# Row standard deviation of an 8192 x 8192 matrix: bn_stats on VectorE for part of each row, and last rows in falling pieces

## Chip, cores, metric

The kernel runs on one core of one Trainium2 chip. The metric is the time of the device in microseconds, of one execution. The profile is of one execution; its span is 1.7 to 2.2 us shorter than the measured time, and all times inside a run are counted from the start of that span.

## The reference

```python
x = np.random.randn(8192, 8192).astype(np.float32)
np.std(x, axis=1)          # 8192 results
```

268 MB must be read, and 32 KB are written.

## The kernel before

Row `p*64 + i` of x lies in partition p of row tile i, so that a tile is 128 rows which are 64 rows (2 MiB) apart in memory, and each partition gets one run of 32 KB. VectorE sums the tile, ScalarE squares and sums it in two passes. The last tile is loaded in two halves. "Row 61" below is row tile 61 of 0 to 63.

```python
    xrows = x.rearrange("(p i) m -> i p m", p=P, i=I)      # I = 64, C = 8192
    rows = [(i, [0, C]) for i in range(I - 1)]             # (shortened)
    rows.append((I - 1, [0, CS, C]))                       # CS = 4096
    xpool = ctx.enter_context(tc.tile_pool(name="xtiles", bufs=5))
    ...
    def do_row(i, cuts):
        asum, asq, base = (sumA, sqA, 0) if i < NB else (sumB, sqB, NB)
        xt = xpool.tile([P, C], FP32, name="xt")
        for ci in range(len(cuts) - 1):
            c0, c1 = cuts[ci], cuts[ci + 1]
            nc.sync.dma_start(out=xt[:, c0:c1], in_=xrows[i][:, c0:c1])
            nc.vector.reduce_sum(out=asum[:, i - base, ci:ci + 1], in_=xt[:, c0:c1], ...)
            ...
                nc.scalar.activation(out=dummy[:, 0:step], in_=xt[:, s0:s0 + step], func=Square,
                                     accum_out=asq[:, i - base, ci + si:ci + si + 1])
    # rows 0 to 61: variance on GpSimd, square root and store while rows 62 and 63 run
    # rows 62 and 63: four small VectorE operations, square root, store on the ScalarE queue
```

Of the kernel before, what the change touches and what calls it, by code (L numbers as in the profile page):

```python
# [1 line left out]

# [4 lines left out]

FP32 = mybir.dt.float32


@with_exitstack
def kernel(
    ctx: ExitStack,
    tc: tile.TileContext,
    x: bass.AP,
    out: bass.AP,
):
    nc = tc.nc
    P = nc.NUM_PARTITIONS  # L20
    R, C = x.shape
    I = R // P
    N = float(C)
    inv_n = 1.0 / N
    CS = C // 2

    xrows = x.rearrange("(p i) m -> i p m", p=P, i=I)
    out_pi = out.rearrange("(p i) -> p i", p=P)

    NB = I - 2  # L30
    rows = []
    for i in range(I - 1):
        rows.append((i, [0, C]))
    rows.append((I - 1, [0, CS, C]))

    xpool = ctx.enter_context(tc.tile_pool(name="xtiles", bufs=5))
    stats = ctx.enter_context(tc.tile_pool(name="stats", bufs=1))
    psum = ctx.enter_context(tc.tile_pool(name="psumdump", bufs=1, space=bass.MemoryType.PSUM))

    dummy = psum.tile([P, CS], FP32)  # L40

    NT = I - NB
    sumA = stats.tile([P, NB, 4], FP32)
    sqA = stats.tile([P, NB, 4], FP32)
    sumB = stats.tile([P, NT, 4], FP32)
    sqB = stats.tile([P, NT, 4], FP32)
    nc.vector.memset(sumB, 0.0)  # L47
    nc.vector.memset(sqB, 0.0)  # L48
    invn_t = stats.tile([P, 1], FP32)
    nc.vector.memset(invn_t, inv_n)  # L50

    def do_row(i, cuts):
        asum, asq, base = (sumA, sqA, 0) if i < NB else (sumB, sqB, NB)
        xt = xpool.tile([P, C], FP32, name="xt")
        for ci in range(len(cuts) - 1):
            c0, c1 = cuts[ci], cuts[ci + 1]
            nc.sync.dma_start(out=xt[:, c0:c1], in_=xrows[i][:, c0:c1])  # L57
            nc.vector.reduce_sum(  # L58
                out=asum[:, i - base, ci:ci + 1],
                in_=xt[:, c0:c1],  # L60
                axis=mybir.AxisListType.X,
            )
            nsub = (c1 - c0 + CS - 1) // CS
            step = (c1 - c0) // nsub
            for si in range(nsub):
                s0 = c0 + si * step
                nc.scalar.activation(  # L67
                    out=dummy[:, 0:step],
                    in_=xt[:, s0:s0 + step],
                    func=mybir.ActivationFunctionType.Square,  # L70
                    accum_out=asq[:, i - base, ci + si:ci + si + 1],
                )

    vA = stats.tile([P, NB], FP32)

    for (i, cuts) in rows:
        do_row(i, cuts)
        if i == NB - 1:
            tsqA = stats.tile([P, NB], FP32)
            nc.gpsimd.tensor_add(tsqA, sqA[:, :, 0], sqA[:, :, 1])  # L80
            t0 = stats.tile([P, NB], FP32)
            nc.gpsimd.tensor_mul(t0, sumA[:, :, 0], sumA[:, :, 0])  # L82
            nc.gpsimd.tensor_mul(t0, t0, invn_t.to_broadcast((P, NB)))  # L83
            nc.gpsimd.tensor_sub(vA, tsqA, t0)  # L84

    tsqB = stats.tile([P, NT], FP32)
    nc.vector.reduce_sum(out=tsqB, in_=sqB, axis=mybir.AxisListType.X)  # L87
    tsumB = stats.tile([P, NT], FP32)
    nc.vector.reduce_sum(out=tsumB, in_=sumB, axis=mybir.AxisListType.X)  # L89
    m2 = stats.tile([P, NT], FP32)  # L90
    nc.vector.scalar_tensor_tensor(  # L91
        out=m2, in0=tsumB, scalar=inv_n, in1=tsumB,
        op0=mybir.AluOpType.mult, op1=mybir.AluOpType.mult,
    )
    vB = stats.tile([P, NT], FP32)
    nc.vector.tensor_sub(vB, tsqB, m2)  # L96

    stdA = stats.tile([P, NB], FP32)
    nc.scalar.activation(out=stdA, in_=vA,  # L99
                         func=mybir.ActivationFunctionType.Sqrt, scale=inv_n)  # L100
    nc.sync.dma_start(out=out_pi[:, 0:NB], in_=stdA)
    stdB = stats.tile([P, NT], FP32)
    nc.scalar.activation(out=stdB, in_=vB,  # L103
                         func=mybir.ActivationFunctionType.Sqrt, scale=inv_n)
    nc.scalar.dma_start(out=out_pi[:, NB:I], in_=stdB)


# [1 line left out]
_INS = ['x']  # L109
_OUTS = [((8192,), 'float32')]  # L110


# [23 lines left out]
```

## Time and profile before

The median was 642.8 us (642.4 to 643.3, three runs).

| what | value | from |
|---|---|---|
| load queue's share of the 16 DMA engines | 97.9% | table of queues |
| rate from 66 to 560 us | 432 GB/s | table of windows |
| one row tile lands every | 9.71 us | landings in the trace |
| VectorE per row / ScalarE per row | 8.69 / 7.5 us | groups of instructions |
| last load lands / last work ends / span ends | 630.4 / 638.5 / 641.0 us | trace, timeline |

These lines are from the profile page of the kernel before. The rows of digits and rates cut the span into 40 equal slices; a queue's line has its packets, megabytes and share of the 16 engines; a group's line has the count, then busy us and mean ns of one, then the idle time before it and what ended it.

```profile
span 641.0 us, 576 instructions
...
GB/s 339 413 419 405 429 433 433 431 432 429 431 433 433 431 429 431 433 433 431 429 431 425 429 428 436 433 430 431 427 438 431 431 431 427 438 431 431 429 422 88
...
q1 hardware_dynamic: 9504, 268.47, 97.9%
q14 instruction: 5, 0.04, 0.0%
...
DMA xt<-in_x_dram 80%; DVE sumA L58 16%; DVE sumB L58 2%; SPq L57 0%; ACT stdB L103 0%; DVE vB L96 0%; DVE m L91 0%; DVE tsumB L89 0%; DVE tsqB L87 0%; DVEq L58 0%
...
L58 DVE TENSOR_REDUCE sumA<-xt 128x1 f32<-128x8192 f32 x62 | 538.5, 8686 | 79.8 <-DMA xt<-in_x_dram 79.8
L67 ACT ACTIVATE dummy<-xt 128x4096 f32<-128x4096 f32 x128 | 459.2, 3587 | 156.1 <-DMA xt<-in_x_dram 154.0
...
```

The rate is flat from the fifth slice on, both compute engines wait for the load in every row, and the load has 80% of the chain of waits. So the load sets the pace. The first four slices (64 us) are slower.

The end of the same kernel in the timeline (start, duration, engine, line, operation):

```profile
...
620.38 17.34 DVE L58 TENSOR_REDUCE sumB<-xt 128x1 f32<-128x8192 f32 x3 [1.10 <-DMA xt<-in_x_dram]
...
631.83 3.59 ACT L67 ACTIVATE dummy<-xt 128x4096 f32<-128x4096 f32 x1
...
637.64 0.15 DVE L87 TENSOR_REDUCE tsqB<-sqB 128x2 f32<-128x8 f32 x1
...
638.34 0.20 ACT L103 ACTIVATE stdB<-vB 128x2 f32<-128x2 f32 x1 [2.80 <-DVE vB L96]
638.58 0.37 ACTq L105 DMA_DIRECT2D out_dram<-stdB  x1
```

The last load lands at 630.4 us, but VectorE is still busy with one row and two halves (17.34 us from 620.38) and reaches 637.7. That backlog is what a better split of the work can remove.

### The profile page before, as it was taken

The page shows a single profiled execution, that of the slowest core. Times are in us where ns is not written, and L with a number is a line of the kernel's source. Part 1 is how long each engine was busy: PE and PEld are TensorE (multiplying, and loading weights), DVE is VectorE, ACT ScalarE, POOL GpSimd, SP SyncE. Part 2 cuts the span into 40 slices and gives each one's busy share as a digit, 9 for nine tenths or more (in the row PEclk, how much of TensorE's full clock was granted, in tenths as well). Part 3 has the DMA queues.
Part 4 walks back from the last instruction along what each step waited for, and adds up shares of the span by engine and source line. Part 5 has one row for each costly group of instructions (what it writes and reads, how often), then busy time and mean ns, then how long its engine had stood idle before and what let it go on. Part 6 is the DMA issues. An engine that isn't in the chain of part 4 may idle for free.

```text
span 641.0 us, 576 instructions
## 1 busy us (share of the span) xinstructions
DVE 556.5 (87%) x72; ACT 477.9 (75%) x260; POOL 1.4 (0%) x8
## 2 busy tenths in 40 slices
DVE  1889889889889898898898898898898988988988
ACT  1767778778778778777787787787787787777886
POOL 0000000000000000000000000000000000000000
DMA  8999999999999999999999999999999999999992
GB/s 339 413 419 405 429 433 433 431 432 429 431 433 433 431 429 431 433 433 431 429 431 425 429 428 436 433 430 431 427 438 431 431 431 427 438 431 431 429 422 88
DMA packets 9653, 268.51 MB, mean 419 GB/s; under 512 B 1328, under 2 KB 1328, under 8 KB 1328
## 3 DMA queue, kind: packets, MB, share of 16 engines
q1 hardware_dynamic: 9504, 268.47, 97.9%
q14 instruction: 5, 0.04, 0.0%
q10 hardware_dynamic: 144, 0.00, 0.0%
HBM read 268.44 MB, written 0.03 MB: 419 GB/s over the span
## 4 chain that ended last, share of the span: by engine, by line
DMA 80%; DVE 19%; issue 1%; SPq 0%; ACT 0%; DVEq 0%
DMA xt<-in_x_dram 80%; DVE sumA L58 16%; DVE sumB L58 2%; SPq L57 0%; ACT stdB L103 0%; DVE vB L96 0%; DVE m L91 0%; DVE tsumB L89 0%; DVE tsqB L87 0%; DVEq L58 0%
## 5 line engine op out<-in xcount | busy, mean ns | idle before, releaser
L58 DVE TENSOR_REDUCE sumA<-xt 128x1 f32<-128x8192 f32 x62 | 538.5, 8686 | 79.8 <-DMA xt<-in_x_dram 79.8
L67 ACT ACTIVATE dummy<-xt 128x4096 f32<-128x4096 f32 x128 | 459.2, 3587 | 156.1 <-DMA xt<-in_x_dram 154.0
L67 ACT ACTIVATION_READ_ACCUMULATOR dummy<-xt 128x1 f32 x128 | 24.0, 187 | 0.0
L58 DVE TENSOR_REDUCE sumB<-xt 128x1 f32<-128x4096 f32 (+1 forms) x3 | 17.3, 5835 | 1.1 <-DMA xt<-in_x_dram 1.1
L103 ACT ACTIVATE stdB<-vB 128x2 f32<-128x2 f32 x1 | 0.2, 204 | 2.8 <-DVE vB L96 2.8
L67 ACT ACT_TABLE_LOAD x1 | 1.3, 1283 | 0.7 <-PEq L120 0.7
L80 POOL TENSOR_TENSOR tsqA<-sqA 128x62 f32<-128x62 f32 x1 | 0.3, 296 | 617.7 <-ACT dummy L67 617.7
L99 ACT ACT_TABLE_LOAD x1 | 1.3, 1283 | 0.0
L99 ACT ACTIVATE stdA<-vA 128x62 f32<-128x62 f32 x1 | 0.3, 257 | 1.0 <-POOL vA L84 1.0
L47 DVE MEMSET sumB<- 128x8 f32 x1 | 0.1, 65 | 0.8 <-PEq L120 0.8
L84 POOL TENSOR_TENSOR vA<-tsqA,t 128x62 f32<-128x62 f32 x1 | 0.3, 317 | 0.1
L82 POOL TENSOR_TENSOR t<-sumA 128x62 f32<-128x62 f32 x1 | 0.3, 295 | 0.9 <-DVE sumA L58 0.9
L83 POOL TENSOR_TENSOR t<-t,invn_t 128x62 f32<-128x62 f32 x1 | 0.3, 291 | 0.1
L96 DVE TENSOR_TENSOR vB<-tsqB,m 128x2 f32<-128x2 f32 x1 | 0.2, 161 | 0.0
L91 DVE SCALAR_TENSOR_TENSOR m<-tsumB 128x2 f32<-128x2 f32 x1 | 0.2, 160 | 0.0
L89 DVE TENSOR_REDUCE tsumB<-sumB 128x2 f32<-128x8 f32 x1 | 0.2, 161 | 0.0
L87 DVE TENSOR_REDUCE tsqB<-sqB 128x2 f32<-128x8 f32 x1 | 0.1, 149 | 0.0
L120 POOL MEMSET const-bfloat16-1.0<- 128x1 bf16 x1 | 0.1, 103 | 0.0
L120 POOL MEMSET const-uint8-127<- 128x1 uint8 x1 | 0.1, 103 | 0.0
L120 POOL MEMSET const-float32-0.0<- 128x1 f32 x1 | 0.1, 99 | 0.2 <-issue 0.2
L120 POOL MEMSET const-float32-1.0<- 128x1 f32 x1 | 0.1, 99 | 0.0
L48 DVE MEMSET sqB<- 128x8 f32 x1 | 0.1, 65 | 0.0
(1 smaller groups left out, 0.1 us busy)
## 6 DMA issues: line engine op xcount, KB each, us to landing
xt<-in_x_dram SPq DMA_DIRECT2D x63, 4096.0 KB, 39.8
xt<-in_x_dram SPq DMA_DIRECT2D x2, 2048.0 KB, 37.6
out_dram<-stdA SPq DMA_DIRECT2D x1, 31.0 KB, 9.8
out_dram<-stdB ACTq DMA_DIRECT2D x1, 1.0 KB, 1.4
```

The source lines that it names most:

```text
L58: nc.vector.reduce_sum(out=asum[:, i - base, ci:ci + 1], in_=xt[:, c0:c1], axis=mybir.AxisListType.X,)
L67: nc.scalar.activation(out=dummy[:, 0:step], in_=xt[:, s0:s0 + step], func=mybir.ActivationFunctionType.Square, accum_out=asq[:, i - base, ...
L80: nc.gpsimd.tensor_add(tsqA, sqA[:, :, 0], sqA[:, :, 1])
L82: nc.gpsimd.tensor_mul(t0, sumA[:, :, 0], sumA[:, :, 0])
L83: nc.gpsimd.tensor_mul(t0, t0, invn_t.to_broadcast((P, NB)))
L84: nc.gpsimd.tensor_sub(vA, tsqA, t0)
L89: nc.vector.reduce_sum(out=tsumB, in_=sumB, axis=mybir.AxisListType.X)
L91: nc.vector.scalar_tensor_tensor(out=m2, in0=tsumB, scalar=inv_n, in1=tsumB, op0=mybir.AluOpType.mult, op1=mybir.AluOpType.mult,)
L96: nc.vector.tensor_sub(vB, tsqB, m2)
L99: nc.scalar.activation(out=stdA, in_=vA, func=mybir.ActivationFunctionType.Sqrt, scale=inv_n)
L103: nc.scalar.activation(out=stdB, in_=vB, func=mybir.ActivationFunctionType.Sqrt, scale=inv_n)
L120: nc = _bacc.Bacc("TRN2", target_bir_lowering=False, num_devices=1)
```

## The change

The intent: bn_stats and bn_aggr give mean and variance in one VectorE pass, so that the columns can be divided; VectorE takes 5120 of them, ScalarE makes two passes over 3072. No engine then has a backlog at the end, and the last row comes in falling pieces, so that little work is left behind the last byte. Each end piece has its own buffer, so that its load is issued early (between 581 and 618 us in the trace of the changed kernel, the last one 13 us before its first report). (The diffs in this document are shortened to the lines that carry the change; some comments were added.)

```diff
-    xpool = ctx.enter_context(tc.tile_pool(name="xtiles", bufs=5))
+    ACT_ROW = 3072
+    pieces = [(i, 0, C, ACT_ROW) for i in range(I - 2)]
+    pieces += [(I - 2, 0, C // 2, ACT_ROW // 2), (I - 2, C // 2, C // 2, ACT_ROW // 2)]
+    for n, a in ((2048, 512), (2048, 512), (2048, 512), (1024, 0), (512, 0), (256, 0), (256, 0)):
+        pieces.append((LAST, c0, n, a)); c0 += n
+    bulk = ctx.enter_context(tc.tile_pool(name="bulk", bufs=4))     # full rows
+    ends = ctx.enter_context(tc.tile_pool(name="ends", bufs=1))     # a tile for each end piece
 ...
-            nc.vector.reduce_sum(out=asum[...], in_=xt[:, c0:c1], axis=X)
+        for d0 in range(a, n, F):                                   # F = 512
+            nc.vector.bn_stats(out=bn[:, k * SD:(k + 1) * SD], in_=xt[:, d0:d1])
+        nc.scalar.activation(out=dump[:, :a], in_=xt[:, :a], func=Square, accum_out=q_act[...])
+        nc.scalar.activation(out=dump[:, :a], in_=xt[:, :a], func=Copy, accum_out=s_act[...])
+            nc.vector.bn_aggr(out=agg[:, r, :], in_=bn)             # once a row
 ... (GpSimd joins both parts: 11 operations for rows 0 to 62, 7 for the last row)
+    nc.vector.bn_aggr(out=agg[:, LAST, :], in_=last_bn)
+    nc.scalar.activation(out=stdl, in_=agg[:, LAST, 1:2], func=Sqrt)
+    nc.scalar.dma_start(out=out_pi[:, LAST:I], in_=stdl)
```

More of the change, by code (lines that the diff above doesn't have):

```diff
@@ L9 @@
 FP32 = mybir.dt.float32
+ACTF = mybir.ActivationFunctionType
+ALU = mybir.AluOpType
 @with_exitstack
@@ L23 @@
     N = float(C)
-    inv_n = 1.0 / N
-    CS = C // 2
-    xrows = x.rearrange("(p i) m -> i p m", p=P, i=I)
+    F = nc.vector.BN_STATS_FMAX
+    SD = nc.vector.BN_STATS_DIM
+    LAST = I - 1
+    xr = x.rearrange("(p i) m -> p i m", p=P, i=I)
     out_pi = out.rearrange("(p i) -> p i", p=P)
-    NB = I - 2
-    rows = []
-    for i in range(I - 1):
-        rows.append((i, [0, C]))
-    rows.append((I - 1, [0, CS, C]))
-    xpool = ctx.enter_context(tc.tile_pool(name="xtiles", bufs=5))
+    ACT_ROW = 3072
@@ L37 @@
+    pieces = [(i, 0, C, ACT_ROW) for i in range(I - 2)]
+    pieces += [(I - 2, 0, C // 2, ACT_ROW // 2), (I - 2, C // 2, C // 2, ACT_ROW // 2)]
+    c0 = 0
+    for n, a in ((2048, 512), (2048, 512), (2048, 512), (1024, 0), (512, 0), (256, 0), (256, 0)):
+        pieces.append((LAST, c0, n, a))
+        c0 += n
+    N_D = float(C - ACT_ROW)
+    bulk = ctx.enter_context(tc.tile_pool(name="bulk", bufs=4))
+    ends = ctx.enter_context(tc.tile_pool(name="ends", bufs=1))
     stats = ctx.enter_context(tc.tile_pool(name="stats", bufs=1))
+    bnp = ctx.enter_context(tc.tile_pool(name="bnp", bufs=3))
@@ L38 @@
     psum = ctx.enter_context(tc.tile_pool(name="psumdump", bufs=1, space=bass.MemoryType.PSUM))
-    dummy = psum.tile([P, CS], FP32)
-    NT = I - NB
-    sumA = stats.tile([P, NB, 4], FP32)
-    sqA = stats.tile([P, NB, 4], FP32)
-    sumB = stats.tile([P, NT, 4], FP32)
-    sqB = stats.tile([P, NT, 4], FP32)
-    nc.vector.memset(sumB, 0.0)
-    nc.vector.memset(sqB, 0.0)
-    invn_t = stats.tile([P, 1], FP32)
-    nc.vector.memset(invn_t, inv_n)
-    def do_row(i, cuts):
-        asum, asq, base = (sumA, sqA, 0) if i < NB else (sumB, sqB, NB)
-        xt = xpool.tile([P, C], FP32, name="xt")
-        for ci in range(len(cuts) - 1):
-            c0, c1 = cuts[ci], cuts[ci + 1]
-            nc.sync.dma_start(out=xt[:, c0:c1], in_=xrows[i][:, c0:c1])
-            nc.vector.reduce_sum(
-                out=asum[:, i - base, ci:ci + 1],
-                in_=xt[:, c0:c1],
-                axis=mybir.AxisListType.X,
-            )
-            nsub = (c1 - c0 + CS - 1) // CS
-            step = (c1 - c0) // nsub
-            for si in range(nsub):
-                s0 = c0 + si * step
-                nc.scalar.activation(
-                    out=dummy[:, 0:step],
-                    in_=xt[:, s0:s0 + step],
-                    func=mybir.ActivationFunctionType.Square,
-                    accum_out=asq[:, i - base, ci + si:ci + si + 1],
-                )
@@ L74 @@
-    vA = stats.tile([P, NB], FP32)
-    for (i, cuts) in rows:
-        do_row(i, cuts)
-        if i == NB - 1:
-            tsqA = stats.tile([P, NB], FP32)
-            nc.gpsimd.tensor_add(tsqA, sqA[:, :, 0], sqA[:, :, 1])
-            t0 = stats.tile([P, NB], FP32)
-            nc.gpsimd.tensor_mul(t0, sumA[:, :, 0], sumA[:, :, 0])
-            nc.gpsimd.tensor_mul(t0, t0, invn_t.to_broadcast((P, NB)))
-            nc.gpsimd.tensor_sub(vA, tsqA, t0)
-    tsqB = stats.tile([P, NT], FP32)
-    nc.vector.reduce_sum(out=tsqB, in_=sqB, axis=mybir.AxisListType.X)
@@ L88 @@
-    tsumB = stats.tile([P, NT], FP32)
-    nc.vector.reduce_sum(out=tsumB, in_=sumB, axis=mybir.AxisListType.X)
-    m2 = stats.tile([P, NT], FP32)
-    nc.vector.scalar_tensor_tensor(
-        out=m2, in0=tsumB, scalar=inv_n, in1=tsumB,
-        op0=mybir.AluOpType.mult, op1=mybir.AluOpType.mult,
-    )
-    vB = stats.tile([P, NT], FP32)
-    nc.vector.tensor_sub(vB, tsqB, m2)
-    stdA = stats.tile([P, NB], FP32)
-    nc.scalar.activation(out=stdA, in_=vA,
-                         func=mybir.ActivationFunctionType.Sqrt, scale=inv_n)
@@ L101 @@
-    nc.sync.dma_start(out=out_pi[:, 0:NB], in_=stdA)
-    stdB = stats.tile([P, NT], FP32)
-    nc.scalar.activation(out=stdB, in_=vB,
-                         func=mybir.ActivationFunctionType.Sqrt, scale=inv_n)
-    nc.scalar.dma_start(out=out_pi[:, NB:I], in_=stdB)
+    dump = psum.tile([P, ACT_ROW], FP32)
+    agg = stats.tile([P, I, 2], FP32)
+    s_act = stats.tile([P, I, 3], FP32)
+    q_act = stats.tile([P, I, 3], FP32)
+    nc.gpsimd.memset(s_act, 0.0)
+    nc.gpsimd.memset(q_act, 0.0)
@@ new lines, with load @@
+    warm = stats.tile([P, 1], FP32)
+    nc.vector.memset(warm, 1.0)
+    nc.scalar.activation(out=warm, in_=warm, func=ACTF.Sqrt)
+    n_last = sum(-(-(n - a) // F) for r, _, n, a in pieces if r == LAST)
+    a_last = float(sum(a for r, _, n, a in pieces if r == LAST))
+    last_bn = stats.tile([P, 3 + n_last * SD], FP32)
+    def load(pi):
+        r, c0, n, _ = pieces[pi]
+        if n == C:
+            xt = bulk.tile([P, C], FP32, name="xt")
+        else:
+            xt = ends.tile([P, n], FP32, name=f"xe{pi}")
+        nc.sync.dma_start(out=xt, in_=xr[:, r, c0:c0 + n])
+        return xt
@@ new lines, with g @@
+    tiles = {}
+    bn, k, j = None, 0, 0
+    for pi, (r, c0, n, a) in enumerate(pieces):
+        if n == C:
+            tiles[pi] = load(pi)
+        elif pi not in tiles:
+            for ahead in range(pi, len(pieces)):
+                tiles[ahead] = load(ahead)
+        xt = tiles.pop(pi)
+        if c0 == 0:
+            k, j = 0, 0
+            if r < LAST:
+                bn = bnp.tile([P, (C - ACT_ROW) // F * SD], FP32, name="bn")
+            else:
+                bn = last_bn[:, 3:]
+        for d0 in range(a, n, F):
+            d1 = min(n, d0 + F)
+            nc.vector.bn_stats(out=bn[:, k * SD:(k + 1) * SD], in_=xt[:, d0:d1])
+            k += 1
+        if a:
+            nc.scalar.activation(out=dump[:, :a], in_=xt[:, :a], func=ACTF.Square,
+                                 accum_out=q_act[:, r, j:j + 1])
+            nc.scalar.activation(out=dump[:, :a], in_=xt[:, :a], func=ACTF.Copy,
+                                 accum_out=s_act[:, r, j:j + 1])
+            j += 1
+        if c0 + n == C and r < LAST:
+            nc.vector.bn_aggr(out=agg[:, r, :], in_=bn)
+        if c0 + n == C and r == LAST - 1:
+            B = LAST
+            def g(nm):
+                return stats.tile([P, B], FP32, name=nm)
+            dm, dv = agg[:, 0:B, 0], agg[:, 0:B, 1]
+            ss, qq, t1, t2, t3, t4 = (g(f"g{z}") for z in range(6))
+            nd = stats.tile([P, 1], FP32)
+            nc.gpsimd.memset(nd, N_D)
+            ndb = nd.to_broadcast((P, B))
+            ninv = stats.tile([P, 1], FP32)
+            nc.gpsimd.memset(ninv, 1.0 / N)
+            ninvb = ninv.to_broadcast((P, B))
+            nc.gpsimd.tensor_add(ss, s_act[:, 0:B, 0], s_act[:, 0:B, 1])
+            nc.gpsimd.tensor_add(qq, q_act[:, 0:B, 0], q_act[:, 0:B, 1])
+            nc.gpsimd.tensor_mul(t1, dm, dm)
+            nc.gpsimd.tensor_add(t1, t1, dv)
+            nc.gpsimd.tensor_mul(t1, t1, ndb)
+            nc.gpsimd.tensor_add(t1, t1, qq)
+            nc.gpsimd.tensor_mul(t2, dm, ndb)
+            nc.gpsimd.tensor_add(t2, t2, ss)
+            nc.gpsimd.tensor_mul(t3, t2, t2)
+            nc.gpsimd.tensor_mul(t3, t3, ninvb)
+            nc.gpsimd.tensor_sub(t4, t1, t3)
+            std = stats.tile([P, B], FP32)
+            nc.scalar.activation(out=std, in_=t4, func=ACTF.Sqrt, scale=1.0 / N)
+            nc.sync.dma_start(out=out_pi[:, 0:B], in_=std)
+        if r == LAST and pi + 1 < len(pieces) and pieces[pi + 1][3] == 0 and a:
+            sl = stats.tile([P, 2], FP32)
+            an = stats.tile([P, 1], FP32)
+            nc.gpsimd.memset(an, 1.0 / a_last)
+            nc.gpsimd.memset(last_bn[:, 0:1], a_last)
+            nc.gpsimd.tensor_add(sl[:, 0:1], s_act[:, r, 0:1], s_act[:, r, 1:2])
+            nc.gpsimd.tensor_add(sl[:, 0:1], sl[:, 0:1], s_act[:, r, 2:3])
+            nc.gpsimd.tensor_add(sl[:, 1:2], q_act[:, r, 0:1], q_act[:, r, 1:2])
+            nc.gpsimd.tensor_add(sl[:, 1:2], sl[:, 1:2], q_act[:, r, 2:3])
+            nc.gpsimd.tensor_mul(last_bn[:, 1:2], sl[:, 0:1], an)
+            m2 = stats.tile([P, 1], FP32)
+            nc.gpsimd.tensor_mul(m2, last_bn[:, 1:2], sl[:, 0:1])
+            nc.gpsimd.tensor_sub(last_bn[:, 2:3], sl[:, 1:2], m2)
@@ L109 @@
+    nc.vector.bn_aggr(out=agg[:, LAST, :], in_=last_bn)
+    stdl = stats.tile([P, 1], FP32)
+    nc.scalar.activation(out=stdl, in_=agg[:, LAST, 1:2], func=ACTF.Sqrt)
+    nc.scalar.dma_start(out=out_pi[:, LAST:I], in_=stdl)
 _INS = ['x']
```

## The prediction

> **What bounds the kernel now.** The load of x. The DMA table gives the load queue 97.9% of the span on the 16 engines; the table of windows reads 431 GB/s from 66 to 620 us, where the Trainium skill ("DMA: Bandwidth & Descriptors", Where 436 GB/s comes from) puts the fabric's ceiling at 435; the trace agrees to 1%. A row tile (4.19 MB) lands every 9.72 us. VectorE needs 8.69 of them and ScalarE about 7.5 (two passes of 3.59 us, each with a 0.19 us accumulator read), so both wait for DMA every row (the list of waits: VectorE 79.8 us, ScalarE 154 us in total). The chain of waits puts 80% on the load; its other 16% (reduction of the row) is only the release of a buffer with three to four loads still queued, so it costs nothing.
>
> What is exposed is the end. In the timeline row 62 lands at 620.3, the last half row about 630.4, but VectorE then still works off 8.69 + 2 x 4.41 us and ends at 637.7; four small operations and the square root take it to 638.5, the store and the end to 641.0.
>
> **What the change does.** Steady state: VectorE does ten bn_stats of 512 and one bn_aggr, ScalarE two passes of 3072. From the two reductions (8686 ns for 8192, 4409 for 4096) one element costs 1.044 ns and an instruction up to 0.13 us; estimate 0.6 to 0.67 us per bn_stats, if it takes one element per cycle like the reduction, 6.2 to 6.9 us per row. ScalarE from its 3.59 us for 4096: about 2.9 us each, 5.8 per row. Both stay under 9.72, so the gain of about 2 us per row is not on the path: worth nothing in 62 rows. Four row buffers for five: a buffer comes free some 6.5 us after landing, with over two loads (20 us) queued; no stall. All end pieces have their own buffers and are queued early.
>
> Tail, all estimates: pieces of row 63 land at about 622.8, 625.3, 627.8, 629.0, 629.6, 630.0, 630.4, perhaps 0.3 us later for more and smaller transfers. VectorE: row 62 done 623.6, third 2048 piece done 629.6, then 2048 columns that are all its own: done about 632.1. ScalarE: row 62 done 623.5; in its order the square root of the 63 rows stands before its second piece of row 63 and waits for eleven GpSimd operations (0.37 us apart in the trace of before), until about 627.5; two more pieces at about 1.5 us end near 630.8; the last four GpSimd operations about 632.0. bn_aggr, square root, store and end (2.66 us from square root to end, as before): 635.2. So 641.0 becomes about 635.2 in the profile, 5.8 us less: all of it in the tail.
>
> **Prediction.** 637.0 us, 8 in 10 between 635.0 and 639.8. Faster by over 2%: 0.03; within 2%: 0.94; slower by over 2%: 0.03.
>
> **What would show it.** Right: rows still land every 9.7 us; window rate 430 GB/s; VectorE busy falls to about 410 us, ScalarE's to about 370, and their waits for DMA grow by as much; time from the last landing to the square root falls from about 8 to about 2 us; ScalarE idles some 2.5 us in front of the 63-row square root. Wrong: a row period of over 10 us, load queue under 96%.
>
> **What would make it wrong.** bn_stats at two cycles per element (11 us per row) would make VectorE the bound, about 10% slower. Four buffers might starve single DMA engines. The start (410 GB/s from 14 to 66 us, 2.6 us lost) may differ with other buffers. Small pieces may land later than their bytes say. None of these can bring 2% faster.

## More of the kernel before

In the table of queues, q14 (instructions) has five packets. The trace also holds, for every load, 16 reports that a share of it is done, which are read here as one from each of the 16 DMA engines. A tile is usable at the last of them. For row 61 the fifteenth report came at 610.35 us and the last at 610.58.

## The result

The changed kernel took 646.85 us (646.45 to 648.39, four runs), against 642.62 us of the kernel before: the ratio is 1.0076 (95% interval 1.0058 to 1.0095). A ratio here is the mean time of one kernel's fast runs over that of the other's of the same rounds, so it is not quite the ratio of the medians. The change made the kernel 0.8% slower; 0.9% faster had been predicted.

The page of the changed kernel, the same kinds of lines:

```profile
span 644.7 us, 1255 instructions
...
GB/s 335 411 427 425 433 433 433 430 435 431 430 429 437 427 431 433 433 434 425 433 433 419 429 436 425 431 435 433 429 429 435 432 431 431 433 429 431 427 326 84
...
q1 hardware_dynamic: 10368, 268.47, 98.3%
q14 instruction: 11, 0.08, 0.0%
...
L88 DVE BATCH_NORM_STATS2 bn<-xt 128x6 f32<-128x512 f32 x620 | 373.9, 678 | 216.6 <-DMA xt<-in_x_dram 216.6
L91 ACT ACTIVATE dump<-xt 128x3072 f32<-128x3072 f32 x62 | 169.6, 2735 | 260.9 <-DMA xt<-in_x_dram 260.9
...
L97 DVE BATCH_NORM_AGGREGATE agg<-bn 128x2 f32<-128x60 f32 x63 | 26.8, 426 | 2.2
...
```

The engines did what was asked: VectorE's busy time fell from 556.5 to 415.4 us and ScalarE's from 477.9 to 366.7. The load's rate in the middle is the same. Two things differ: the slice before the last has 326 GB/s instead of 422, and q14 has 11 packets instead of 5 (ten of them are 8 KB of instructions).

The end of the changed kernel in its timeline:

```profile
...
626.32 3.07 DVE L88 BATCH_NORM_STATS2 bn<-xe 128x6 f32<-128x512 f32 x5 [3.47 <-DMA xe<-in_x_dram]
...
630.67 1.88 DVE L88 BATCH_NORM_STATS2 last_bn<-xe 128x6 f32<-128x512 f32 x3 [0.83 <-DMA xe<-in_x_dram]
...
634.70 1.88 DVE L88 BATCH_NORM_STATS2 last_bn<-xe 128x6 f32<-128x512 f32 x3 [2.15 <-DMA xe<-in_x_dram]
...
637.18 4.31 DVE L88 BATCH_NORM_STATS2 last_bn<-xe 128x6 f32<-128x512 f32 x8 [0.60 <-DMA xe<-in_x_dram]
...
641.60 0.55 DVE L139 BATCH_NORM_AGGREGATE agg<-last_bn 128x2 f32<-128x87 f32 x1
642.18 0.20 ACT L141 ACTIVATE stdl<-agg 128x1 f32<-128x1 f32 x1 [3.47 <-DVE agg L139]
642.42 0.37 ACTq L142 DMA_DIRECT2D out_dram<-stdl  x1
```

VectorE waits in front of each of these four groups of pieces (3.47, 0.83, 2.15 and 0.60 us; the last group holds four pieces); the backlog of rows is gone, and the last eight bn_stats end 1.8 us after the last landing. The work behind the last landing shrank as planned: the last piece lands at 639.7 us (landings in the trace) and the last square root begins at 642.2. But the kernel before had its last landing at 630.4. So the sum is: 5.5 us won behind the last landing (638.54 - 630.35 = 8.19 before, 642.38 - 639.73 = 2.65 now), 9.38 us lost in front of it, 3.8 net; the spans differ by 3.7.

Where those 9.4 us lie is read from the landings. This is a table from the traces, not a view of the profile. "Fetches" are packets of 8 KB on the instruction queue within the span; the "15th" and "last" are the last two of the 16 reports for row 61, and the time between them is called the lag of the last engine. Each line is one execution, and e5 and e7 ran on another chip, so differences within a line say more than those between lines.

```
kernel                fetches   row 61: 15th    last    last load landed    span
before                      5         610.35  610.58              630.35   641.0
changed                    10         610.35  613.42              639.73   644.7
e1_wide_end_loads          10         610.64  614.76              635.29   643.0
e2_pitch63                 10         606.74  610.04              630.78   641.6
e3_tiny_copies             10         609.88  614.00              634.88   646.2
e4_four_buffers             5         609.43  609.99              630.12   640.4
e5_few_instructions         5         611.03  611.45              637.86   642.3
e7_before_pitch63           5         606.61  606.99              627.19   637.6
```

Row 61 is 2.8 us later in the changed kernel, and it is one engine that is late: the fifteenth report is where it was.

That it is there to 0.01 us is partly luck. The slow start differs from trace to trace, and row 5 had landed at 66.1 us before and at 65.0 in the changed kernel. From row 5 to row 61, the start left out, the last report took 544.4 us before and 548.4 now: 4.0 us lost, of which the start gave 1.2 back. In the traces of the table this stretch is 544.4 to 545.3 us with five fetches and 547.9 to 549.5 with ten. The mean of the 16 reports hardly shows it: 544.5 us before, 544.9 in the changed kernel, 544.5 in e3 (545.9 at most, in e1). The engines together lost little; one of them fell 3 to 4 us behind.

The rest of the 9.4 us, 26.3 us from row 61 to the last landing instead of 19.8, falls in the last two rows.

The late engine does not fall back steadily. In the chain of waits of the changed kernel one stretch of DMA covers three to four rows (start, us, what):

```profile
...
457.00 6.04 DVE bn L88 x10
463.03 0.02 SPq L68
463.06 0.03 issue
463.09 32.76 DMA xt<-in_x_dram
...
501.96 33.71 DMA xt<-in_x_dram
...
```

The undisturbed stretches have 32.74 to 32.76 us, such as the one at 463.09; the one at 501.96 has about one more. Around that moment the table of queues for the window 505 to 520 us has a packet of instructions:

```profile
...
q1 hardware_dynamic: 215, 6.42, 99.7%
q14 instruction: 1, 0.01, 0.1%
...
```

The trace's moments of such packets against the distance between two landings of rows (9.71 us in nearly all) and the lag of the last engine behind the fifteenth:

```
changed kernel: fetch at   166.58   284.10   379.02, 382.12, 392.40   509.94   624.19, 624.94
next long distance, us      10.48    10.69                    10.68    10.69   (end pieces)
last engine's lag after      0.76     1.75                     2.05     3.03   6.15
```

Each step of about 1 us follows a fetch, and the steps add up in one single report, so they fell on one engine. (At row 38 the lag was down to 1.15 us, as the fifteenth report had fallen back after the fetches at 379.02 and 382.12; so the next step to 2.05 is 0.9. The lag of 6.15 is no measure of a fetch: it is the second half of row 62, which the late engine still loads while the others are at the short pieces. Two earlier fetches, at 56.4 and 128.4 us, left steps of under 0.3 us; one long distance, 10.17 us at 358.9, has no fetch before it, holds all engines alike, and stands in the kernel before too, with 9.97 at 357.8.) In this trace the engine that has lost a microsecond does not win it back (the lag stays at 1.75 to 1.83 us from row 28 to row 37, at 3.03 to 3.07 from row 51 to row 61), and a tile is only ready when the slowest engine is done. In the kernel before, too, one of the 16 reports falls back by 0.7 to 1.0 us after the fetches at 138.4, 382.1 and 420.1 us, but each time one from the middle of the order, so the row lands no later. So in these traces a fetch delays the rows where it hits the engine that is already last, or throws another one behind it.

### The profile page after: what moved, and what is told of

The parts are those of the page before. It is cut to its first block, busy times and chain, and to the rows that moved or that the text cites. A ratio compares the mean times of both kernels' runs of the same rounds, so it can differ in the third digit from the quotient of the medians.

```text
span 644.7 us, 1255 instructions
## 1 busy us (share of the span) xinstructions
DVE 415.4 (64%) x709; ACT 366.7 (57%) x272; POOL 5.2 (1%) x28
## 3 DMA queue, kind: packets, MB, share of 16 engines
q1 hardware_dynamic: 10368, 268.47, 98.3%
## 4 chain that ended last, share of the span: by engine, by line
DMA 83%; DVE 15%; another core or an unknown queue 0%; SPq 0%; issue 0%; ACT 0%; DVEq 0%
DMA xt<-in_x_dram 76%; DVE bn L88 14%; DMA xe<-in_x_dram 8%; DVE last_bn L88 1%; SPq L68 0%; DVE agg L139 0%; ACT stdl L141 0%; DVEq L139 0%
## 5 line engine op out<-in xcount | busy, mean ns | idle before, releaser
L88 DVE BATCH_NORM_STATS2 bn<-xt 128x6 f32<-128x512 f32 x620 | 373.9, 678 | 216.6 <-DMA xt<-in_x_dram 216.6
L91 ACT ACTIVATE dump<-xt 128x3072 f32<-128x3072 f32 x62 | 169.6, 2735 | 260.9 <-DMA xt<-in_x_dram 260.9
L93 ACT ACTIVATE dump<-xt 128x3072 f32<-128x3072 f32 x62 | 169.6, 2735 | 1.9
L97 DVE BATCH_NORM_AGGREGATE agg<-bn 128x2 f32<-128x60 f32 x63 | 26.8, 426 | 2.2
L91 ACT ACTIVATION_READ_ACCUMULATOR dump<-xt 128x1 f32 x62 | 11.6, 186 | 0.0
L93 ACT ACTIVATION_READ_ACCUMULATOR dump<-xt 128x1 f32 x62 | 11.5, 186 | 0.0
L88 DVE BATCH_NORM_STATS2 last_bn<-xe 128x6 f32<-128x512 f32 (+1 forms) x14 | 8.1, 641 | 3.6 <-DMA xe<-in_x_dram 3.6
L91 ACT ACTIVATE dump<-xe 128x512 f32<-128x512 f32 (+1 forms) x5 | 4.7, 943 | 8.2 <-DMA xe<-in_x_dram 8.1
L88 DVE BATCH_NORM_STATS2 bn<-xe 128x6 f32<-128x512 f32 x10 | 6.1, 674 | 3.5 <-DMA xe<-in_x_dram 3.5
L93 ACT ACTIVATE dump<-xe 128x512 f32<-128x512 f32 (+1 forms) x5 | 4.7, 943 | 0.2
L91 ACT ACTIVATION_READ_ACCUMULATOR dump<-xe 128x1 f32 x5 | 0.9, 186 | 0.0
L93 ACT ACTIVATION_READ_ACCUMULATOR dump<-xe 128x1 f32 x5 | 0.9, 185 | 0.0
```

Source lines behind the costliest of these rows:

```text
L88: nc.vector.bn_stats(out=bn[:, k * SD:(k + 1) * SD], in_=xt[:, d0:d1])
L91: nc.scalar.activation(out=dump[:, :a], in_=xt[:, :a], func=ACTF.Square, accum_out=q_act[:, r, j:j + 1])
L93: nc.scalar.activation(out=dump[:, :a], in_=xt[:, :a], func=ACTF.Copy, accum_out=s_act[:, r, j:j + 1])
L97: nc.vector.bn_aggr(out=agg[:, r, :], in_=bn)
```

## The experiments

Theory F: the change executes more instructions (1255 instead of 576 in the profile); they are fetched in blocks over the same DMA engines, most often over the same one, at about 1 us of that engine for each block. Theory P: transfers with short runs per partition, 8 KB and less, at a distance of 2 MiB between partitions, make the 16 engines slow one another. (The runs test the length and the distance, not whether it is one another that they slow.) Rival B: four row buffers instead of five starve single engines. Rival N: short runs, or many transfers, cost as such, whatever the addresses. (The text for e1 calls yet another rival S: the fetches alone delay the end.)

The Trainium skill has something on both: "DMA: Bandwidth & Descriptors", Queues, rings and completion order, names queue row 14 as the runtime's own, for refills among others; and the same page's Latency and other measured facts has a row on copies that are slower when rows lie a large power of two apart, with the aliasing of memory channels as an unverified cause. Neither says what it does to this kernel, so it was tried.

e1 to e4 ran on one chip together; the kernel before took 642.04 us there (641.06 to 642.66).

### e1: the last row in two wide transfers

```diff
-            for ahead in range(pi, len(pieces)):
-                tiles[ahead] = load(ahead)
+            for h in (0, C // 2):          # row 63: two loads of 4096, the seven pieces are views
+                big = ends.tile([P, C // 2], FP32, name=f"xl{h}")
+                nc.sync.dma_start(out=big, in_=xr[:, LAST, h:h + C // 2])
```

> The changed kernel, but the last row is loaded as two transfers of 4096 columns; the work on it is cut into the same pieces as before. Theory P (narrow pieces: engines reading 8 KB runs together slow one another): the last landing moves from 639.7 us to about 636 us (626.3 for row 62 plus two of 4.87 us, as the kernel before has them), packets of 8 KB at 0.46 us are gone; the time falls only by about 1 us, because eight bn_stats now stand behind the last landing. Rival S (the instruction fetches alone delay the end): last landing stays within 1 us of 639.7. Both: rows 0 to 61 land as in the changed kernel, row 61 at about 613.4.

The time was 642.89 us, ratio 1.0021 (1.0001 to 1.0040). From row 61 to the last landing there were 20.5 us instead of 26.3. So the narrow transfers cost 5.8 us, and that comes back although the fetches (ten) and the lag of the last engine (4.1 us at row 61) stayed. By the ratios the time fell by 0.55%, some 3.5 us, where about 1 us had been expected; the profiled execution (644.8 us, the slowest of the four) has a span only 1.7 us shorter than that of the changed kernel. Rival S, the fetches alone, falls. The last landing at 635.3 is 0.7 under what was expected. Row 61 landed at 614.8, 1.3 us later than in the changed kernel, so one trace differs from another by about that much; the lag of the last engine is the steadier sign (3.1 to 4.1 us in all four traces with ten fetches, 0.2 to 0.6 in all four with five, worked out from the table above).

### e2: another distance between partitions, the same pieces

```diff
-    xr = x.rearrange("(p i) m -> p i m", p=P, i=I)
+    M = P * LAST                                             # 8064 rows, 63 in a partition
+    xm = x[0:M, :].rearrange("(p i) m -> p i m", p=P)
+    xl = x[M:R, :]                                           # last tile: 128 adjacent rows
```

> The changed kernel with rows laid out otherwise: the first 8064 rows with 63 per partition (distance between partitions 63 rows instead of 64, 2.02 instead of 2.10 MB), the last row tile is the 128 rows left, next to one another. The pieces keep their sizes; the result is right. Theory P in its address form (a distance of 2 MiB makes the 16 engines meet in the same part of memory): packets of 8 KB take about 0.31 us, last landing about 635 us, the time 642 us or less; perhaps the slow first 66 us get faster too. Rival (small packets or many transfers cost as such): packets of 8 KB stay at 0.46 us and the last landing near 639.7 us.

The packets of 8 KB took 0.316 us in the mean; in the changed kernel they took 0.488 (median 0.464, the 0.46 of the expectations). The last load landed at 630.8 us, 9 us earlier than in the changed kernel, with the same pieces and the same ten fetches. Both numbers were as theory P has it (the landing even 4 us better, because the start became faster too, see e7). The moments at which the pieces are issued are nearly the same (577.7 to 615.0 us here, 581.1 to 618.3 in the changed kernel), so late issues are not what slows them. But this run changes two distances: the full rows are 63 rows apart, and the last tile's are adjacent. The time was 643.34 us, ratio 1.0023 (1.0006 to 1.0039): not the 642 or less that was expected. The chain of waits ends at 633.4, and the reason for the rest is in the table of issues:

```profile
...
out_dram<-stdl ACTq DMA_DIRECT2D x1, 0.5 KB, 7.4
```

The last store took 7.4 us, where it takes 1.4 us in the changed kernel. In this layout it writes 128 words of 4 bytes that lie next to one another; in the changed kernel, whose page has

```profile
...
out_dram<-stdl ACTq DMA_DIRECT2D x1, 0.5 KB, 1.4
```

the 128 words lie 64 words apart.

### e3: more instructions in the kernel before

```diff
+            for z in range(10):
+                nc.vector.tensor_copy(tiny[:, i, z:z + 1], xt[:, c0 + z:c0 + z + 1])
```

> The kernel before plus ten one-column copies per transfer on VectorE, 650 instructions more, nothing else. VectorE needs about 9.4 us per row, still under 9.72. Theory F (each block of 128 instructions is fetched by a DMA that costs one DMA engine about 1 us, and the slowest engine paces the rows): about 5 fetches more, row 61 lands 2 to 4 us later than at 610.6, the last of the 16 engines falls 2 to 3 us behind the others, time 2 to 4 us more. Rival B (four buffers instead of five): row 61 stays at 610.6.

The time was 647.13 us, ratio 1.0083 (1.0067 to 1.0098). The fetches went from five to ten, at nearly the moments of the changed kernel (167.1, 284.6, 393.1 and 510.6 us), and the rows after them landed 10.66 to 10.70 us apart. Row 61 landed 3.4 us later than in the kernel before, and its last engine lagged by 4.1 us. With the transfers, the buffers and the reduction untouched, added VectorE instructions alone produced the pattern. That it is their fetching, and not their execution, is read from the times: the copies are the same in every row, and only the rows behind a fetch are late. 650 instructions brought five fetches, about 130 to each. The time rose by 5.1 us, more than the 2 to 4 expected, and the span by 5.2; the 1.8 us beyond the late row are the ten copies each behind the last row and its two halves (about 0.6 us each), which lengthen VectorE's backlog.

### e4: four buffers in the kernel before

```diff
-    xpool = ctx.enter_context(tc.tile_pool(name="xtiles", bufs=5))
+    xpool = ctx.enter_context(tc.tile_pool(name="xtiles", bufs=4))
```

> The kernel before with four row buffers instead of five, nothing else. Theory F: row 61 lands at 610.6 plus or minus 0.5 us, time the same within 0.5 us. Rival B (four buffers starve single DMA engines): row 61 lands about 3 us later, the time rises by about 3 us.

The time was 641.65 us, ratio 0.9996 (0.9982 to 1.0011); row 61 landed at 609.99, as expected. Rival B falls.

The instruction queue of the two, from their pages, e3 first:

```profile
...
q14 instruction: 10, 0.08, 0.0%
...
```

```profile
...
q14 instruction: 5, 0.04, 0.0%
...
```

### e5: fewer instructions in the changed kernel

e5, e6, e7 and e8 ran together on another chip; the kernel before took 645.66 us there (643.61 to 648.68), so only ratios are compared from one group to the next.

```diff
+        if n == C and r < LAST - 2:          # rows 0 to 60 as in the kernel before
+            nc.vector.reduce_sum(out=s_act[:, r, 0:1], in_=xt, axis=X)
+            for h in (0, 1):
+                nc.scalar.activation(out=dump, in_=xt[:, h*C//2:(h+1)*C//2], func=Square, accum_out=q_act[:, r, h:h+1])
+            continue
```

> The changed kernel with rows 0 to 60 done as in the kernel before (one sum over 8192 on VectorE, two square passes of 4096 on ScalarE), rows 61 to 63 and all transfers as in the changed kernel. Theory F (instruction fetches): at most 6 blocks fetched during the run instead of 10, row 61 lands at 610.0 to 611.5 us instead of 613.4, the last engine less than 1.2 us behind the fifteenth. Theory P: packets of 8 KB still take 0.46 us and the last landing is still 4 us or more later than 630.4. Time 640 to 643 us. If row 61 stays near 613.4, the fetches are not the cause.

There were five fetches, row 61 landed at 611.45 us, and its last engine lagged by 0.42 us instead of 3.07 us. The pieces still came slowly: the 8 KB packets took 0.507 us in the mean, and the last one landed at 637.9. The two causes can be switched separately. From row 61 to the last landing it took 26.4 us, as long as in the changed kernel, so what is lost in the last two rows does not hang on the ten fetches. The time was 646.54 us, ratio 1.0010 (0.9985 to 1.0035): over the 640 to 643 that were expected, but the kernel before, too, took 3.6 us more in this group than in the first.

### e7: another distance in the kernel before

```diff
+    xrows = [x[M:R, :]] + [xm[i] for i in range(I - 1)]      # adjacent rows first, then 63 apart
```

> The kernel before with only the rows laid out otherwise: first the 128 adjacent rows, then 63 rows per partition. Theory P in its address form: the first 66 us lose nothing, rows land every 9.72 us from the first, row 61 lands 3 to 4 us earlier than at 610.6; time about 638.5 us. Rival (the slow start is the engines getting under way, whatever the addresses): no change, 642 us.

The time was 639.02 us (638.95 to 639.34), ratio 0.9891 (0.9871 to 0.9912). The first five rows landed 9.71 us apart; in the kernel before the distances were 11.1, 9.7, 10.3, 10.3 and 10.7. The table of windows for 14 to 66 us, the kernel before first (duration, busy us of the engines, granted clock, DMA share, GB/s):

```profile
...
14.00:66.00 52.00, 43.43 (x5) 37.11 (x20) 0.00 (x0) 1.00 0.99 409
...
```

```profile
...
14.00:66.00 52.00, 46.87 (x6) 40.44 (x23) 0.00 (x0) 1.00 1.00 434
...
```

The DMA share is 99 to 100% in both, so it does not tell how much the busy engines move; only the rate does. At 64 rows the start loses 3.6 us by row 61, with full 32 KB runs too. Why the loss ends there, and the same distance then runs at 432 GB/s, no run shows.

### e8 and e9: narrow transfers in every row

```diff
-            nc.sync.dma_start(out=xt[:, c0:c1], in_=xrows[i][:, c0:c1])
+            for d in range(c0, c1, 2048):
+                nc.sync.dma_start(out=xt[:, d:d + 2048], in_=xrows[i][:, d:d + 2048])
```

e8 has this at 64 rows per partition (the kernel before):

> The kernel before with every row of 8192 columns loaded in four transfers of 2048 columns, the work unchanged. Theory P: packets of 8 KB at a distance of 2 MiB slow one another throughout, 0.4 us or more each instead of 0.31, so that the kernel takes 800 us or more. Rival (8 KB packets are slow only at the end, where the engines run dry unequally): 642 us plus 1 to 5.

e9 has it at 63 rows per partition (e7), later, on the first chip, together with e10:

> The kernel before with rows laid out 63 per partition and every row of 8192 columns loaded in four transfers of 2048 columns. Theory P in its address form: packets of 8 KB take 0.31 us, and the time is 640 us within 5, although the same transfers at 64 rows per partition took 1025.7 us. If narrow transfers cost as such: far over 700 us.

e8 took 1025.7 us and e9 654.2 us, one execution each. The windows from 66 to 560 us, e8 first:

```profile
...
66.00:560.00 494.00, 270.08 (x32) 230.80 (x125) 0.00 (x0) 1.00 0.96 266
...
```

```profile
...
66.00:560.00 494.00, 430.67 (x50) 367.27 (x199) 0.00 (x0) 1.00 1.01 422
...
```

The same transfers run at 266 GB/s with 64 rows per partition and at 422 with 63. The 8 KB packets took 0.473 and 0.314 us. Here the end pieces of another layout play no part, which was the weak point of e2. e9 was to be within 5 us of 640 and missed that by 9: a load of 2048 columns lands every 2.49 us rather than a quarter of 9.71, 2.43, and 256 times 0.06 is 16 us. So rival N has a small share, 2.5% at most (the single execution of e9 also holds seven fetches), against 57% for the distance (1025.7 over 654.2).

### e6 and e10: both findings used

e6 has 63 rows per partition with the adjacent tile first (its results stored after row 0), rows 0 to 60 with few instructions, and the last three as in the changed kernel (the third piece of the last row with 1024 columns on ScalarE).

```diff
+    xm = x[0:M, :].rearrange("(p i) m -> p i m", p=P)         # M = 8064: rows 1 to 63
+    xf = x[M:R, :]                                            # row 0: 128 adjacent rows
+        if n == C and r < LAST - 2:                           # as in e5
+            ...
+                nc.scalar.dma_start(out=of, in_=std0)         # row 0's results, early
-    ... (2048, 512), (2048, 512), (2048, 512), (1024, 0) ...
+    ... (2048, 512), (2048, 512), (2048, 1024), (1024, 0) ...
```

> All three findings used: 63 rows per partition with the 128 adjacent rows done first and stored early, few instructions in the full rows, the last two rows in falling pieces with bn_stats and the ScalarE share. Correct result. Both theories together: packets of 8 KB at 0.31 us, row 61 lands at about 606, last landing about 626.5 us, work ends about 628.5, span about 630.5, time about 632 us, 1.5% under the kernel before. If only one of the two holds: 635 us or more.

It is correct and took 638.98 us, ratio 0.9890 (0.9872 to 0.9908), not 632. The packets of 8 KB were as expected (0.313 us), but rows 2 and 3 landed 12.35 and 12.58 us after the row before: 5.5 us lost just after the store of the 128 adjacent words was issued at 22.9 us. That store took 18.2 us, and in that stretch packets of 32 KB took up to 4.0 us (up to 1.22 in the same stretch of e10). The page of e6 has

```profile
...
out_dram<-std ACTq DMA_DIRECT2D x1, 0.5 KB, 18.2
...
```

e10 turns those results with VectorE and stores four runs of 128 bytes:

```diff
-                nc.scalar.dma_start(out=of, in_=std0)                  # 128 partitions x 4 bytes
+                nc.vector.transpose(turned, std0)                      # 32 x 32 blocks
+                nc.scalar.dma_start(out=of, in_=turned[0:P:32, :])     # 4 partitions x 128 bytes
```

> The combined kernel, but the 128 adjacent results of the first tile are turned by VectorE (32 x 32 blocks) and stored as 4 runs of 128 bytes instead of 128 single words. If the single-word store held up the loads (rows 2 and 3 landed 12.4 and 12.6 us apart, 5.5 us lost): rows land every 9.72 us from the first, last landing about 627 us instead of 632.3, span about 631, time about 633 us. If the loss at the start had another cause: 639 us again.

It is correct and took 633.17 us (633.04 to 633.25), ratio 0.9797 (0.9772 to 0.9822) to the kernel before, which took 645.84 us beside it (644.21 to 648.73). The window from 22 to 48 us, e6 first:

```profile
...
22.00:48.00 26.00, 17.69 (x3) 15.30 (x10) 0.49 (x3) 1.00 1.00 339
...
```

```profile
...
22.00:48.00 26.00, 23.40 (x4) 20.88 (x12) 0.39 (x2) 1.00 1.00 434
...
```

The last load landed at 627.0 us as expected. So the single words were what held up the loads there. In e7 the same 128 words are stored on the load's own queue behind its last loads; there the way from row 61 to the last landing was 20.2 us, only 0.4 longer than in the kernel before, so the loss is not the same wherever such a store stands. The end of e10 in its timeline:

```profile
...
624.41 3.78 DVE L111 BATCH_NORM_STATS2 last_bn<-xe 128x6 f32<-128x512 f32 x7 [0.43 <-DMA xe<-in_x_dram]
...
628.29 0.52 DVE L162 BATCH_NORM_AGGREGATE agg<-last_bn 128x2 f32<-128x81 f32 x1
628.85 0.20 ACT L164 ACTIVATE stdl<-agg 128x1 f32<-128x1 f32 x1 [1.79 <-DVE agg L162]
...
```

The kernel before takes 642 us in some calls and 646 in others; the runs with 63 rows per partition (e2, e7, e10) spread by under 0.4 us each, e6 by 1.5. Against the 642.0 of the first group e10 would be 1.4% faster, against its own group 2.0% (1.8 to 2.3), so whether it reaches 2% is open. The chip alone is not the reason for the difference: the first chip gave 642.0 with e1 to e4 and 645.8 with e9 and e10. What makes it was not looked into.

## Why the prediction was wrong

- The bound, the row period and the worth of the saved engine time were right: 9.71 us per row, 431 GB/s from 66 to 560 us, nothing won in the full rows. Busy times came out as said (415.4 us for about 410 on VectorE, 366.7 for about 370 on ScalarE), and so did the durations: ten bn_stats and one bn_aggr took 6.5 us.
- The win behind the last landing was right in size: the square root began 2.5 us after it, where about 2 had been predicted and 8.0 measured before.
- The step that failed most is "pieces of row 63 land at about 622.8, ... 630.4, perhaps 0.3 us later". The last one landed at 639.7, 9.3 us later. Of that, 5.8 us are the narrow transfers at a distance of 2 MiB (e1 gives them back, e2 and e8 with e9 show that the distance does it). The landing was worked out from bytes and the mean rate, and that rate had been measured on runs of 32 KB, and 16 KB in the last tile. "Small pieces may land later than their bytes say" stood among the risks, with a third of a microsecond in the sum.
- The second failed step is that the full rows were taken to cost what they had cost ("worth nothing in 62 rows"), with silence on what more instructions cost. That the saved engine time is worth nothing there was right; but row 61 landed 2.8 us later, 4.0 us lost from row 5 on (3.7 of them in four rows behind fetches) less the 1.2 us of a luckier start. e3 makes this loss with nothing but instructions, e5 takes it away.
- The last 0.8 us of the 9.4 (20.5 us from row 61 to the last landing in e1, 19.8 in the kernel before) are not explained: e4, with five fetches and wide loads, has 20.1, so part of it is the spread from trace to trace.
- The test that the prediction named for this, a period of 9.7 us and 430 GB/s, would have passed: four of 62 rows were 0.8 to 1.0 us too long, and the load queue had 98.3%. A mean over 500 us does not show 4 us.
- "ScalarE idles some 2.5 us in front of the 63-row square root" was wrong (0.3 us); the late pieces left it idle earlier.
- "Four buffers might starve single DMA engines" named a risk that did not show (e4: row 61 at 609.99 us, time the same).

What stays open: why a fetch whose packet takes 0.31 us costs an engine 0.7 to 1.0 us, and why the fetches for VectorE's instructions fall so often on one engine (the trace does not name the engine of a packet). That the 2 MiB distance acts through memory channels is the skill's inference; the runs show the distance, not the channels. Only two distances were tried, 64 and 63 rows, and why 32 KB runs are slow at 64 rows in the first 66 us alone is open.

## What to carry to other kernels

When a load fills the DMA engines, time everything else that uses them: here a fetch of instructions pushed one engine back by about 1 us for the rest of the run, a store of 128 adjacent words held up the loads by 5.5 us, and the slowest engine set the pace. Do not cut a transfer into short runs before looking at how far apart the partitions' rows lie; with a distance of 2 MiB 8 KB runs got 266 GB/s, and one row less per partition gave 422. Compare the landing times of the last full row and of the last piece in both kernels before crediting anything to the end of the kernel.

## What the Trainium skill lacked or had wrong

- "Runtime: NRT & Kernel Launch", Instruction fetch mechanics, calls the cost of crossing a block of instructions "mostly hidden". In this kernel, bound by DMA, a fetch made a row 0.8 to 1.0 us longer each time it hit the slowest engine, and ten fetches instead of five made row 61 3.4 us later (e3). Where a fetch hit another engine, as in the kernel before, the page's word held: no row after the start was more than 0.3 us too long there. The page speaks of 16 KiB blocks; the packets here have 8 KB.
- "DMA: Bandwidth & Descriptors", Latency and other measured facts, gives 164 GB/s per direction for 16 KiB runs between HBM tensors at a distance of 2 MiB. Loads to SBUF with 32 KB runs at that distance got 432 GB/s (only the first 66 us were slow), and 8 KB runs 266; 16 KB runs were tried in the last tile alone, where a packet took 0.616 us, half of the 1.225 of 32 KB. The row does not say that the length of the run decides, nor that one row less (2,064,384 bytes) is enough.
- No page gives the cost of a store of adjacent 4-byte words from 128 partitions: 7.4 us with the loads done (e2), 18.2 us beside them, with 5.5 us lost by the loads (e6). Turned into four runs of 128 bytes it held up no row (e10). Four runs were tried in that one place only.
- "VectorE: DVE Perf Modes" has no figures for bn_stats and bn_aggr: 0.60 us from one bn_stats of 512 columns to the next, 0.43 us for a bn_aggr of 60 numbers and 0.55 us for 87.
